# Modulation columns by a multiply-and-sum over weights with features on partitions, and the first input made tile by tile

## The chip, the cores and the metric

The program runs on one core of a Trainium2 chip. Its time is device microseconds from start to end of one execution; the median of three runs before the change is 1673.4 us (1672.69 to 1673.78). TensorE is PE, VectorE DVE, ScalarE ACT, GpSimd POOL, and SyncE (SP) issues most transfers.

## The reference, cut to what matters

Two transformer-like models run one after the other over one sequence of 256 tokens with 1024 features, all in float32. The first has two layers whose normalised input is scaled and shifted by a modulation made of one conditioning vector c. For each layer six vectors of 1024 features are computed:

```
s      = silu(c)                       # 1024 values
mod[v] = s @ w_ada[:, v] + b_ada[v]    # v = 0..5, each 1024 features
v = 0, 1: shift and scale of the mixer's input
v = 3, 4: shift and scale of the feed-forward's input
v = 2, 5: gate of the branch's result (added as 1 + mod[v])
h      = x * (1 + scale) + shift
```

The input of the first mixer is `x * (1 + mod[1]) + mod[0]`, without a norm. From it q, k and v of two kinds of heads are projected, attention is computed, its result projected by w_o, gated, added and normalised; a gated feed-forward follows; then layer two, and then the second model (two more layers, which the change does not touch).

## The kernel before, in words

All weights are streamed from HBM in tiles of 128 x 1024 floats (512 KB) by SP's queue, in program order. `load` (L224) puts a tile into one of four "raw" buffers and splits it into two float32r parts: ACT casts the high part (L230), VectorE subtracts to get the low part (L239). Each product is three matmuls: high x high, high x low, low x high (`tok`, L260, for a 128-token block; `feat`, L249, and `both`, L305, for features).

w_ada tiles go into four buffers "ra" of their own. A step of `ada_acc` (L606) loads one tile of 128 input features x 1024 output features and adds it, times the 128 values of silu(c) as a per-partition scalar, to an accumulator "acc" (L618, L620). After eight steps acc holds on each partition a part of every output feature's sum. For gate rows (`ada_row`) a matmul with ones sums over partitions and leaves the row on all of them (L647). For shift and scale the features must lie on partitions: `ada_cols` (L627) runs eight matmuls with one column each, acc as the stationary operand (L632, 16 records in the profile), and one small VectorE instruction adds the bias (L633). The steps stand in a list "background", of which one or so is taken out with each `load`, so that they lie between the weights of the mixer and the feed-forward.

The first input has its own code at the start. `first_half` (L800) loads eight tiles that hold 512 features of shift and of scale, sums them on VectorE (L808, L810), runs the eight one-column matmuls (L813), and adds the biases (L815, L816). `first_hT` (L818) makes the four hT tiles of that half (L823 on ACT, L825 on VectorE, split at L243 and L244), and `first_v` (L828) projects them to v with weights v_ab; for these loads every second low part is subtracted by POOL. Then the second half does the same. The four results are copied out of PSUM by VectorE (L854). The order within an engine's queue is chosen when the program is built, from the program order and a scheduler's estimates; each engine runs its queue in that order.

Of the kernel before, what the change touches and what calls it, by code (L numbers as in the profile page):

```python
# [37 lines left out]
LAMBDA_INIT = 0.8 - 0.6 * math.exp(-0.3 * 0)  # L38
TWO_PI = 2.0 * math.pi
# [70 lines left out]
def tile_two_blocks(ctx: ExitStack, tc: tile.TileContext, d: dict, out: bass.AP, upto: int = 99):  # L110
# [489 lines left out]
    with ExitStack() as b1:  # L600
        b1.enter_context(extra_w(XW))
        adap = b1.enter_context(tc.tile_pool(name="adap", bufs=2))
        sc = keep.tile([P, 8], F32, name="sc")
        A.activation(sc, pc("c"), AF.Silu)

        def ada_acc(l, v, then):  # L606
# [3 lines left out]
            def step(k):  # L610
                if k == 0:
                    box.append(adap.tile([P, 1024], F32, tag="acc", name=nm("acc"), bufs=ACCB))
                acc = box[0]
                raw = adap.tile([P, 1024], F32, tag="ra", name=nm("ra"), bufs=RAB)
                last_dma[0] = nc.sync.dma_start(raw, d["w_ada"][l, k, :, v * D:(v + 1) * D])
                with tc.issue_after(last_norm[0].ins) if last_norm[0] else nullcontext():
                    if k == 0:
                        V.tensor_scalar(acc, raw, sc[:, 0:1], None, op0=ALU.mult)  # L618
                    else:
                        V.scalar_tensor_tensor(acc, in0=raw, scalar=sc[:, k:k + 1], in1=acc, op0=ALU.mult, op1=ALU.add)  # L620
                if k == KT - 1:
                    then(acc)
# [177 lines left out]
        def first_half(h, gain, bias):  # L800

            acc = adap.tile([P, 1024], F32, tag="acc", name=nm("acc"), bufs=ACCB)
            for k in range(KT):
                raw = adap.tile([P, 1024], F32, tag="ra", name=nm("ra"), bufs=RAB)
                last_dma[0] = nc.sync.dma_start(
                    raw.rearrange("p (v c) -> p v c", v=2), d["w_ada"][0, k, :, 0:2 * D].rearrange("p (v c) -> p v c", v=2)[:, :, h * 512:(h + 1) * 512])
                if k == 0:
                    V.tensor_scalar(acc, raw, sc[:, 0:1], None, op0=ALU.mult)  # L808
                else:
                    V.scalar_tensor_tensor(acc, in0=raw, scalar=sc[:, k:k + 1], in1=acc, op0=ALU.mult, op1=ALU.add)  # L810
            b = pbank()
            for k in range(KT):
                mm(b[:, k:k + 1], acc[:, k * P:(k + 1) * P], cc("ones")[:, 0:1], start=True, stop=True)  # L813
            c = slice(4 * h, 4 * h + 4)
            V.scalar_tensor_tensor(gain[:, c], in0=b[:, 4:8], scalar=1.0, in1=pc("b_ada", 8 + 4 * h, 4), op0=ALU.add, op1=ALU.add)  # L815
            V.tensor_add(bias[:, c], b[:, 0:4], pc("b_ada", 4 * h, 4))  # L816

        def first_hT(h, xb, hT, gain, bias):  # L818
            for k in range(4 * h, 4 * h + 4):
                i = xb[k // 2][:, (k % 2) * T:(k % 2 + 1) * T]  # L820
                z = np_.tile([P, T], F32, tag="pr", name=nm("h"), bufs=3)
                if k % 2 == 0:
                    A.activation(z, i, AF.Identity, scale=gain[:, k:k + 1], bias=bias[:, k:k + 1])  # L823
                else:
                    V.tensor_scalar(z, i, gain[:, k:k + 1], bias[:, k:k + 1], op0=ALU.mult, op1=ALU.add)  # L825
                split(hT[:, 0, k, :], hT[:, 1, k, :], z)

        def first_v(h, ws, vb, hT):  # L828
            for t in range(2):
                for k in range(4 * h, 4 * h + 4):  # L830
                    tok(vb[t], ws[k // 2 - 2 * h], (k % 2) * 512, hT, k, t, first=k == 0, last=k == KT - 1)
# [3 lines left out]
        gain, bias = keep.tile([P, 8], F32, name="gain"), keep.tile([P, 8], F32, name="bias")  # L835
        pool_share[1] = 0.5
# [5 lines left out]
        for h in range(2):  # L842
            first_half(h, gain, bias)
            first_hT(h, xb, hT, gain, bias)
            if h == 0:
                vab = [[pbank(), pbank()], [bank(), bank()]]
            with tc.issue_after(last_dma[0].ins):
                ws = [[load(d["v_ab"][j][2 * h + i]) for i in range(2)] for j in range(2)]
# [720 lines left out]
def layout(a):  # L1569
# [38 lines left out]
    def inter(q, k):  # L1608
# [4 lines left out]
        "w_ada": a["w_ada"].reshape(2, KT, P, 6 * D), "b_ada": a["b_ada"], "ln_g": a["ln_g"], "ln_b": a["ln_b"],  # L1613
# [47 lines left out]
```

## Time and profile before

| what | value |
|---|---|
| median of three runs | 1673.4 us |
| profiled execution, its own time | 1672.3 us |
| span of the trace within it | 1670.5 us |
| TensorE busy, matmul / weight load | 1609.5 us / 1357.5 us |
| VectorE, ACT, POOL busy | 1254.5, 899.4, 129.7 us |
| one-column matmul records: L813, L632 | 32, 96 |
| mean granted TensorE clock | 0.991 of full speed |

Busy times of matmuls overlap and their ends are modelled, so a full TensorE row says that it had work in hand, and not that it ran at its peak. The chain of waits goes back from the last instruction, at each step to what released it; its pieces in a stretch show which work set the time there. The granted clock of a stretch is 1.00 at 2.4 GHz and 0.50 at 1.2 GHz.

### The profile page before, as it was taken

The page shows a single profiled execution, that of the slowest core. Times are in us where ns is not written, and L with a number is a line of the kernel's source. Part 1 is how long each engine was busy: PE and PEld are TensorE (multiplying, and loading weights), DVE is VectorE, ACT ScalarE, POOL GpSimd, SP SyncE. Part 2 cuts the span into 40 slices and gives each one's busy share as a digit, 9 for nine tenths or more (in the row PEclk, how much of TensorE's full clock was granted, in tenths as well). Part 3 has the DMA queues.
Part 4 walks back from the last instruction along what each step waited for, and adds up shares of the span by engine and source line. Part 5 has one row for each costly group of instructions (what it writes and reads, how often), then busy time and mean ns, then how long its engine had stood idle before and what let it go on. Part 6 is the DMA issues. An engine that isn't in the chain of part 4 may idle for free.

```text
span 1670.5 us, 24925 instructions
## 1 busy us (share of the span) xinstructions
PE 1609.5 (96%) x9156; PEld 1357.5 (81%) x9156; DVE 1254.5 (75%) x2468; ACT 899.4 (54%) x1650; POOL 129.7 (8%) x170
## 2 busy tenths in 40 slices
PE   5899999999999999899999999999999999999998
PEld 4787788878877888688887878888888887778887
DVE  6898988989769766897766897766676667666663
ACT  2465654556446545445556566555565555655552
POOL 1110000000000000286100100000000002000000
PEclk9899999999989999999999999999999999999999
DMA  8877788848726655245554336655375555545550
GB/s 283 333 281 259 242 309 313 310 163 290 253 88 235 235 186 189 98 169 177 193 191 154 118 124 222 234 189 189 124 231 192 192 182 164 177 139 202 190 190 37
DMA packets 103210, 336.14 MB, mean 201 GB/s; under 512 B 15008, under 2 KB 20384, under 8 KB 103088
## 3 DMA queue, kind: packets, MB, share of 16 engines
q1 hardware_dynamic: 102368, 332.54, 57.6%
q10 hardware_dynamic: 720, 2.02, 0.3%
q8 instruction: 71, 1.16, 0.3%
q14 instruction: 51, 0.42, 0.1%
HBM read 332.41 MB, written 2.10 MB: 200 GB/s over the span
## 4 chain that ended last, share of the span: by engine, by line
PE 80%; DVE 10%; DMA 3%; ACT 3%; issue 1%; POOL 1%; SPq 0%; POOLq 0%; ACTq 0%; DVEq 0%
PE p L309 26%; PE p L311 14%; PE a L336 7%; PE a L337 7%; PE a L338 7%; DVE wt L239 3%; PE p L264 3%; PE p L266 3%; PE p L265 2%; PE a L172 2%; PE qk L256 2%; PE qk L257 2%; PE qk L258 2%; ACT wt L230 1%; PE a L479 1%
## 5 line engine op out<-in xcount | busy, mean ns | idle before, releaser
L239 DVE TENSOR_TENSOR wt<-raw,wt 128x512 fp32r<-128x512 f32 (+1 forms) x940 | 675.8, 747 | 146.3 <-ACT wt L230 140.4
L230 ACT CAST wt<-raw 128x1024 fp32r<-128x1024 f32 x512 | 535.9, 1049 | 228.9 <-PE a L338 90.9
L309 PE MATMUL p<-hT,wt 128*128 128x512 f32 x1920 | 484.1, 393 | 0.0
L309 PEld LDWEIGHTS p<-hT,wt 128*128 128x128 f32 x1920 | 352.0, 189 | 68.5 <-issue 1.2
L311 PEld LDWEIGHTS p<-hT,wt 128*128 128x128 f32 x1920 | 262.7, 191 | 18.6 <-issue 0.2
L311 PE MATMUL p<-hT,wt 128*128 128x256 f32 x1920 | 269.3, 283 | 0.0
L336 PE MATMUL a<-wt,r 128*128 128x512 f32 x528 | 206.9, 392 | 0.0
L337 PE MATMUL a<-wt,r 128*128 128x512 f32 x528 | 206.8, 392 | 0.0
L338 PE MATMUL a<-wt,r 128*128 128x512 f32 x528 | 206.1, 390 | 0.0
L264 PE MATMUL p<-wt,hT 128*128 128x512 f32 x352 | 143.8, 411 | 6.1 <-ACT hT L243 5.1
L266 PE MATMUL p<-wt,hT 128*128 128x512 f32 x352 | 141.5, 404 | 2.6 <-DVE hT L244 2.5
L265 PE MATMUL p<-wt,hT 128*128 128x512 f32 x352 | 141.3, 403 | 2.4 <-DVE wt L239 1.5
L315 ACT COPY s<-p 128x256 f32<-128x256 f32 x120 | 44.5, 371 | 165.2 <-PE p L311 165.1
L338 PEld LDWEIGHTS a<-wt,r 128*128 128x128 f32 x528 | 99.2, 188 | 21.4 <-DVE r L244 0.3
L336 PEld LDWEIGHTS a<-wt,r 128*128 128x128 f32 x528 | 99.6, 189 | 18.0
L337 PEld LDWEIGHTS a<-wt,r 128*128 128x128 f32 x528 | 99.5, 189 | 17.1
L315 ACT COPY pr<-p 128x256 f32<-128x256 f32 x120 | 44.5, 371 | 107.9 <-PE p L311 107.8
L316 DVE TENSOR_TENSOR s<-p,s 128x256 f32<-128x256 f32 x120 | 50.8, 423 | 65.9 <-ACT s L315 65.4
L256 PE MATMUL qk<-hT,wt 128*128 128x256 f32 x320 | 94.3, 295 | 0.0
L257 PE MATMUL qk<-hT,wt 128*128 128x256 f32 x320 | 92.9, 290 | 0.0
L258 PE MATMUL qk<-hT,wt 128*128 128x256 f32 x320 | 92.8, 290 | 0.0
L620 DVE SCALAR_TENSOR_TENSOR acc<-ra,sc,acc 128x1024 f32<-128x1024 f32 x70 | 89.3, 1276 | 0.0
(335 smaller groups left out, 1838.4 us busy)
## 6 DMA issues: line engine op xcount, KB each, us to landing
raw<-in_w_ffn_d_dram SPq DMA_DIRECT2D x132, 512.0 KB, 3.3
raw<-in_w_ffn_g_dram SPq DMA_DIRECT2D x120, 512.0 KB, 3.3
raw<-in_w_ffn_u_dram SPq DMA_DIRECT2D x120, 512.0 KB, 3.3
ra<-in_w_ada_dram SPq DMA_DIRECT2D x96, 512.0 KB, 5.2
raw<-in_w_ffn_dram SPq DMA_DIRECT2D x24, 512.0 KB, 3.6
raw<-in_w_ab_dram SPq DMA_DIRECT2D x16, 512.0 KB, 5.6
raw<-in_w_o_dram SPq DMA_DIRECT2D x16, 512.0 KB, 5.4
raw<-in_w_cd_dram SPq DMA_DIRECT2D x16, 512.0 KB, 4.4
```

What stands on the lines that cost most here:

```text
L230: A.copy(w[:, 0, :n], raw[:, :n])
L239: last_part[eng is G] = eng.tensor_sub(w[:, 1, c:c + g], raw[:, c:c + g], w[:, 0, c:c + g])
L256: mm(o, wh, xh, start=first and k == 0, stop=False)
L257: mm(o, wh, xl, start=False, stop=False)
L264: mm(o, xh, w[:, 0, c0:c0 + n], start=first, stop=False)
L265: mm(o, xh, w[:, 1, c0:c0 + n], start=False, stop=False)
L266: last_tok[0] = mm(o, xl, w[:, 0, c0:c0 + n], start=False, stop=last)
L309: mm(o, w[:, 0, k * P:(k + 1) * P], both_parts, start=k == 0, stop=False)
L311: mm(o[:, T:2 * T], w[:, 1, k * P:(k + 1) * P], hT[:, 0, k, :], start=False, stop=k == KT - 1)
L336: mm(o, a[:, 0, tt_(t)], w[:, 0, c], start=m == 0, stop=False)
L337: mm(o, a[:, 0, tt_(t)], w[:, 1, c], start=False, stop=False)
L338: mm(o, a[:, 1, tt_(t)], w[:, 0, c], start=False, stop=m == MT - 1)
```

## The change

silu(c) is also kept as a row "crow": c is read with one transfer to all 128 partitions, and ACT applies Silu over 1024 elements. The host lays the w_ada tiles for shift and scale out with output features on partitions and all 1024 input features along the row. One VectorE instruction (tensor_tensor_reduce) multiplies such a tile by crow, in place, and sums along the row: 128 finished features in one column. `ada_cols` needs no accumulator and no matmul, `ada_row` is as before but for its source's layout. The start goes through the eight feature tiles in order: two sums, one addition of biases, one ACT instruction, cast and subtraction, and after each pair of tiles the matmuls of both v projections, whose weights are now loaded two at a time ahead of the w_ada tiles. POOL subtracts nothing at the start, all four v banks come from one PSUM pool, and ACT copies the results out.

```diff
+        crow = adap.tile([P, 1024], F32, tag="crow", name="crow", bufs=1)
+        nc.scalar.dma_start(crow, d["c_row"].to_broadcast([P, D]))
         A.activation(sc, pc("c"), AF.Silu)
+        A.activation(crow, crow, AF.Silu)
...
+        def ada_dot(l, v, f, o):
+            raw = adap.tile([P, 1024], F32, tag="ra", name=nm("ra"), bufs=RAB)
+            last_dma[0] = nc.sync.dma_start(raw, d["w_ada_col"][l, COLV.index(v), f])
+            with tc.issue_after(last_norm[0].ins) if last_norm[0] else nullcontext():
+                V.tensor_tensor_reduce(raw, raw, crow, 1.0, 0.0, ALU.mult, ALU.add, o)
+
         def ada_cols(l, v, o, plus=0.0):
-            def then(acc):
-                b = pbank()
-                for k in range(KT):
-                    mm(b[:, k:k + 1], acc[:, k * P:(k + 1) * P], cc("ones")[:, 0:1], start=True, stop=True)
-                V.scalar_tensor_tensor(o, in0=b[:, 0:8], scalar=plus, in1=pc("b_ada", (l * 6 + v) * 8, 8),
-                                       op0=ALU.add, op1=ALU.add)
-            ada_acc(l, v, then)
+            def step(f):
+                ada_dot(l, v, f, o[:, f:f + 1])
+                if f == KT - 1:
+                    V.scalar_tensor_tensor(o, in0=o, scalar=plus, in1=pc("b_ada", (l * 6 + v) * 8, 8),
+                                           op0=ALU.add, op1=ALU.add)
+            for f in range(KT):
+                background.append(lambda f=f: step(f))
...
+        def first_hT(k, xb, hT, mod_):
+            for v in range(2):
+                with tc.issue_after(last_dma[0].ins) if last_dma[0] else nullcontext():
+                    ada_dot(0, v, k, mod_[:, v, k:k + 1])
+            V.tensor_add(mod_[:, :, k:k + 1], mod_[:, :, k:k + 1], b01[:, :, k:k + 1])
+            z = np_.tile([P, T], F32, tag="pr", name=nm("h"), bufs=3)
+            A.activation(z, xb[k // 2][:, (k % 2) * T:(k % 2 + 1) * T], AF.Identity,
+                         scale=mod_[:, 1, k:k + 1], bias=mod_[:, 0, k:k + 1])
+            split(hT[:, 0, k, :], hT[:, 1, k, :], z)
...
-        pool_share[1] = 0.5
...
+        vab = [[pbank(), pbank()], [pbank(), pbank()]]
+        for h in range(KT // 2):
+            with tc.issue_after(last_dma[0].ins) if last_dma[0] else nullcontext():
+                ws = [load(d["v_ab"][j][h]) for j in range(2)]
+            for k in (2 * h, 2 * h + 1):
+                first_hT(k, xb, hT, mod_)
             for j in range(2):
-                first_v(h, ws[j], vab[j], hT)
+                for t in range(2):
+                    for k in (2 * h, 2 * h + 1):
+                        tok(vab[j][t], ws[j], (k % 2) * 512, hT, k, t, first=k == 0, last=k == KT - 1)
         for j in range(2):
             for t in range(2):
                 v = kept()
-                V.tensor_copy(v, vab[j][t])
+                A.copy(v, vab[j][t])
```

Three places show how instructions move. The first is VectorE's queue at the start, before, from the last sums of the first half to its first hT (acc: accumulator, ra and raw: weight buffers, wt: split weights):

```order
L810 SCALAR_TENSOR_TENSOR acc_132<-ra_148,sc,acc_132 128x1024
L691 TENSOR_SCALAR mlam<-s_99 128x1
L810 SCALAR_TENSOR_TENSOR acc_132<-ra_151,sc,acc_132 128x1024
L810 SCALAR_TENSOR_TENSOR acc_132<-ra_154,sc,acc_132 128x1024
L815 SCALAR_TENSOR_TENSOR gain<-p_157,prm 128x4
L816 TENSOR_TENSOR bias<-p_157,prm 128x4
L239 TENSOR_TENSOR wt_190<-raw_188,wt_190 128x1024
L244 TENSOR_TENSOR hT_109<-h_168,hT_109 128x256
L825 TENSOR_SCALAR h_172<-a_112,gain,bias 128x256
L825 TENSOR_SCALAR h_180<-a_113,gain,bias 128x256
```

and after, from the second multiply-and-sum on (it stands as two ISA rows, the second of which reads the sum; crow: silu(c) as a row, mod: finished columns, b: biases):

```order
L638 ISA ra_154,mod_114<-ra_154,crow 128x1024
L638 ISA mod_114 128x1
L704 TENSOR_SCALAR mlam<-s_102 128x1
L638 ISA ra_162,mod_114<-ra_162,crow 128x1024
L638 ISA mod_114 128x1
L818 TENSOR_TENSOR mod_114<-mod_114,b_113 128x2
L638 ISA ra_165,mod_114<-ra_165,crow 128x1024
L638 ISA mod_114 128x1
L246 TENSOR_TENSOR hT_112<-h_158,hT_112 128x256
L818 TENSOR_TENSOR mod_114<-mod_114,b_113 128x2
L241 TENSOR_TENSOR wt_199<-raw_197,wt_199 128x1024
L246 TENSOR_TENSOR hT_112<-h_169,hT_112 128x256
```

The first hT subtraction stood behind eight steps over a whole half, and now stands behind four sums and two weight subtractions; the later weight subtractions stand between the sums of the next tiles.

The second is ACT's queue at the start, which also issues transfers (prm: columns of parameters, cst: constants, sc: silu(c) as columns, g: lambda's row). Before:

```order
L150 DMA prm<-in_cols_dram 128x348
L152 DMA cst<-in_consts_dram 128x1284
L155 DMA x<-in_x_dram 128x1024 x2
L604 ACT_TABLE_LOAD
L604 ACTIVATE sc<-prm 128x8
L682 DMA g_96<-in_lam_dram 128x256
L1050 ACT_TABLE_LOAD
L1050 ACTIVATE s_7013<-prm 128x16
L688 ACTIVATE s_98<-s_98 128x2
L230 CAST wt_190<-raw_188 128x1024
L823 ACTIVATE h_168<-a_112,bias,gain 128x256
```

and after:

```order
L152 DMA prm<-in_cols_dram 128x348
L154 DMA cst<-in_consts_dram 128x1284
L157 DMA x<-in_x_dram 128x1024 x2
L608 DMA crow<-in_c_row_dram 128x1024
L609 ACT_TABLE_LOAD
L609 ACTIVATE sc<-prm 128x8
L695 DMA g_99<-in_lam_dram 128x256
L610 ACTIVATE crow<-crow 128x1024
L232 CAST wt_143<-raw_141 128x1024
L232 CAST wt_148<-raw_146 128x1024
```

crow's transfer stands behind x and ahead of lambda's, and its Silu ahead of the first weight cast.

The third is TensorE's queue in the feed-forward of layer one, around a modulation column's matmuls (p: PSUM banks of gate and up, a: those of the down projection, r: the gated activations). Before:

```order
L309 MATMUL p_2617<-hT_1375,wt_2612 128x512 x8
L311 MATMUL p_2617<-hT_1375,wt_2612 128x256 x8
L632 MATMUL p_2664<-cst,acc_2414 128x1 x8
L336 MATMUL a_1833<-wt_2676,r_2577 128x512
L337 MATMUL a_1833<-wt_2676,r_2577 128x512
```

and after:

```order
L311 MATMUL p_2585<-hT_1353,wt_2580 128x512 x8
L313 MATMUL p_2585<-hT_1353,wt_2580 128x256 x8
L338 MATMUL a_1802<-wt_2635,r_2545 128x512
L339 MATMUL a_1802<-wt_2635,r_2545 128x512
L340 MATMUL a_1802<-wt_2635,r_2545 128x512
```

The group on acc is gone, and the matmuls of the down projection follow the gate and up at once.

## Rows read from the trace of the kernel before

**Rows 1.** page, parts 1 and 4: busy us (share) xinstructions; shares of the chain

```profile
PE 1609.5 (96%) x9156; PEld 1357.5 (81%) x9156; DVE 1254.5 (75%) x2468; ACT 899.4 (54%) x1650; POOL 129.7 (8%) x170
...
PE 80%; DVE 10%; DMA 3%; ACT 3%; issue 1%; POOL 1%; SPq 0%; POOLq 0%; ACTq 0%; DVEq 0%
```

**Rows 2.** busy by stage: PE, PEld, DVE, ACT, POOL, granted clock, DMA share, GB/s

```profile
0.00:66.40 66.40, 37.88 (x146) 30.92 (x147) 44.02 (x55) 18.74 (x29) 11.18 (x8) 0.92 0.83 297
66.40:113.00 46.60, 45.87 (x363) 41.68 (x362) 43.91 (x108) 27.17 (x72) 3.98 (x3) 1.00 0.84 306
113.00:190.00 77.00, 75.78 (x437) 60.03 (x436) 69.91 (x163) 48.10 (x112) 3.41 (x3) 1.00 0.74 253
190.00:360.00 170.00, 169.58 (x900) 144.77 (x899) 146.12 (x251) 87.39 (x147) 0.95 (x1) 1.00 0.81 286
```

**Rows 3.** chain of waits, 0 to 120 us: start, us, what

```profile
2.24 12.95 DMA ra<-in_w_ada_dram
...
22.00 3.58 PE p L813 x16
...
66.14 0.23 PE a L266
```

**Rows 4.** the same in short stretches

```profile
4.00:6.00 2.00, 0.00 (x0) 0.00 (x0) 0.66 (x4) 1.06 (x3) 0.00 (x0) 1.00 1.06 416
...
32.00:34.00 2.00, 1.74 (x8) 1.10 (x6) 2.00 (x2) 0.00 (x0) 2.00 (x1) 1.00 0.00 0
...
46.00:48.00 2.00, 1.19 (x6) 1.19 (x6) 0.76 (x1) 1.04 (x1) 0.00 (x0) 0.50 1.03 422
...
56.00:58.00 2.00, 2.00 (x10) 1.41 (x8) 2.00 (x2) 0.93 (x1) 1.94 (x1) 1.00 0.88 296
...
476.00:477.00 1.00, 1.00 (x4) 0.73 (x3) 0.26 (x4) 0.47 (x2) 0.00 (x0) 0.50 0.00 0
```

**Rows 5.** timeline, VectorE, 73.9 to 78 us: start, duration, engine, line, operation

```profile
73.96 0.29 DVE L493 CUSTOM_DVE_ANT_0 g<-a,g 128x128 f32<-128x128 f32 x1 [1.01 <-PE a L479]
...
74.18 0.42 DVE L493 CUSTOM_DVE_ANT_0 g<-a,g 128x256 f32<-128x256 f32 x1
74.53 0.09 DVE L493 DVE_READ_ACCUMULATOR2_ANT s<- 128x1 f32 x1
74.53 1.22 DVE L239 TENSOR_TENSOR wt<-raw,wt 128x1024 fp32r<-128x1024 f32 x1
75.66 0.16 DVE L496 RECIPROCAL s<-s 128x2 f32<-128x2 f32 x1
...
76.28 1.28 DVE L620 SCALAR_TENSOR_TENSOR acc<-ra,sc,acc 128x1024 f32<-128x1024 f32 x1
77.48 0.16 DVE L496 RECIPROCAL s<-s 128x2 f32<-128x2 f32 x1
```

**Rows 6.** VectorE's groups by line and form: xcount | busy, mean ns

```profile
L244 DVE TENSOR_TENSOR hT<-h,hT 128x256 fp32r<-128x256 f32 x8 | 10.3, 1303 | 0.0
...
L618 DVE TENSOR_SCALAR acc<-ra,sc 128x1024 f32<-128x1024 f32 x10 | 7.4, 744 | 0.0
```

**Rows 7.** timeline, all engines, start of the program

```profile
14.37 0.36 DVE L686 TENSOR_TENSOR g<-g 128x64 f32<-128x64 f32 x2 [0.48 <-DMA g<-in_lam_dram]
...
21.81 1.04 ACT L230 CAST wt<-raw 128x1024 fp32r<-128x1024 f32 x1 [4.81 <-DMA raw<-in_v_ab_dram]
...
25.94 0.56 ACT L823 ACTIVATE h<-a,bias,gain 128x256 f32<-128x256 f32 x1 [3.09 <-DVE bias L816]
...
26.97 0.43 DVE L244 TENSOR_TENSOR hT<-h,hT 128x256 fp32r<-128x256 f32 x1
...
46.81 3.57 PE L813 MATMUL p<-cst,acc 128*128 128x1 f32 x16 [5.26 <-DVE acc L810]
```

**Rows 8.** chain of waits: first and last of the six L632 groups

```profile
119.64 1.68 PE p L632 x16
...
470.60 2.27 PE p L632 x16
```

More of the change, by code (lines that the diff above doesn't have):

```diff
@@ L38 @@
 LAMBDA_INIT = 0.8 - 0.6 * math.exp(-0.3 * 0)
+COLV = (0, 1, 3, 4)
 TWO_PI = 2.0 * math.pi
@@ L614, in step @@
                 raw = adap.tile([P, 1024], F32, tag="ra", name=nm("ra"), bufs=RAB)
-                last_dma[0] = nc.sync.dma_start(raw, d["w_ada"][l, k, :, v * D:(v + 1) * D])
+                last_dma[0] = nc.sync.dma_start(raw, d["w_ada_row"][l, v // 3, k])
                 with tc.issue_after(last_norm[0].ins) if last_norm[0] else nullcontext():
@@ L798, in log1p @@
             V.tensor_sub(o, o, e)
[L800 to L831, printed above, removed]
+        def first_hT(k, xb, hT, mod_):
[7 more added lines that the diff above has]
+            split(hT[:, 0, k, :], hT[:, 1, k, :], z)
@@ L834, in tile_two_blocks @@
         hT = new_hT()
-        gain, bias = keep.tile([P, 8], F32, name="gain"), keep.tile([P, 8], F32, name="bias")
-        pool_share[1] = 0.5
+        b01, mod_ = (keep.tile([P, 2, 8], F32, name=n) for n in ("b01", "mod01"))
+        V.tensor_copy(b01[:, 0, :], pc("b_ada", 0, 8))
+        V.tensor_scalar(b01[:, 1, :], pc("b_ada", 8, 8), 1.0, None, op0=ALU.add)
         xb = [bank() for _ in range(4)]
@@ L841, in tile_two_blocks @@
                 transpose(xb[k // 2][:, o:o + P], x[:, t, k * P:(k + 1) * P])
[L842 to L848, printed above, removed]
+        vab = [[pbank(), pbank()], [pbank(), pbank()]]
[4 more added lines that the diff above has]
+                first_hT(k, xb, hT, mod_)
             for j in range(2):
-                first_v(h, ws[j], vab[j], hT)
+                for t in range(2):
+                    for k in (2 * h, 2 * h + 1):
+                        tok(vab[j][t], ws[j], (k % 2) * 512, hT, k, t, first=k == 0, last=k == KT - 1)
         for j in range(2):
@@ L1552, in _tok, with _ada @@
     return np.ascontiguousarray(w.reshape(4, 2, P, 512).transpose(0, 2, 1, 3)).reshape(4, P, 1024)
+def _ada(w, vs):
+    return np.ascontiguousarray(w.reshape(2, KT, P, 6, D).transpose(0, 3, 1, 2, 4)[:, list(vs)])
 def _first(g, u):
@@ L1612, in layout @@
         "consts": consts, "sel": sel, "band": band, "cols": cols, "x": a["x"].reshape(2, P, D),
-        "w_ada": a["w_ada"].reshape(2, KT, P, 6 * D), "b_ada": a["b_ada"], "ln_g": a["ln_g"], "ln_b": a["ln_b"],
+        "c_row": a["c"].reshape(1, D), "w_ada_row": _ada(a["w_ada"], (2, 5)),
+        "w_ada_col": np.ascontiguousarray(_ada(a["w_ada"], COLV).reshape(2, 4, D, KT, P).transpose(0, 1, 3, 4, 2)), "b_ada": a["b_ada"], "ln_g": a["ln_g"], "ln_b": a["ln_b"],
         "rel": rel, "lam": a["diff_lambda"].reshape(1, 256),
```

## Prediction, made before the changed kernel ran

> **What bounds the kernel now.** I read the page's busy shares and chain first, then the stages, then the start in small pieces. The page shows TensorE busy 96% of the span and carrying 80% of the chain that ended last; VectorE carries 10% [rows 1]. The stages show where TensorE isn't full: up to 66.4 us it is busy only 37.88 us, and behind that it is busy nearly all the time, 45.87 of 46.60, 75.78 of 77.00, 169.58 of 170.00 us, with VectorE almost as full in the first of these (43.91 of 46.60) [rows 2]. So two questions decide: how early the first projection (v_ab) ends, and which TensorE work goes away behind it.
>
> The chain of the start shows why TensorE waits: 12.95 us for first weights of w_ada, then VectorE sums, then 16 one-column matmul records of L813 (3.58 us), and all of this again for the second half of the features (46.81 us, [rows 7]); the last matmul of the v projection ends at 66.14 + 0.23 = 66.4 us [rows 3]. The transfers don't run through: 416 GB/s at 4 to 6 us, nothing at 32 to 34 us, when the four buffers "ra" wait for VectorE and the four "raw" for the second half. The second half runs at a granted clock of 0.50 (1.2 GHz) after TensorE had idled 5.26 us [rows 7], and only at 56 us is it back at 1.00 (2.4 GHz) [rows 4].
>
> **The start, step by step.** Both L813 groups, both waits for a whole half and the four POOL subtractions go. In their place each of the 8 feature tiles needs two 512 KB tiles and two multiply-and-sum instructions; then one small addition, one ACT instruction, a cast and a subtraction give that tile's hT. Bytes stay the same but for crow (512 KB). What is late next is VectorE, in order:
>
> - Cost of a multiply-and-sum over 1024 elements: not in the trace, but the same instruction exists in the softmax (L493). 128 elements start 0.22 us before the next instruction (73.96 to 74.18), 256 elements 0.35 us (74.18 to 74.53), so 0.13 us per 128 columns: 0.35 + 6 × 0.13 = 1.13 us. The reading of its sum starts with the next instruction, at the same 74.53. The nearest whole row, scalar_tensor_tensor over 1024, takes a step of 1.20 us (76.28 to 77.48) [rows 5]. I take 1.20; from above 1.28 + 0.08 = 1.36, if the reading stood alone.
> - VectorE's list for the start is 16 × 1.20 = 19.2 us; 8 weight subtractions of 1.13 (74.53 to 75.66) [rows 5] = 9.0; 8 hT subtractions of 0.43 [rows 7] = 3.4 (the 1.30 us mean of this form in the start [rows 6] holds those that ran beside POOL's subtractions, and POOL has none now); 8 additions of 0.15 = 1.2; lambda and the like 1.4; the first ada_row step 0.74 [rows 6]. Sum 35.0 us.
> - It begins when crow is there. crow stands on ACT's queue behind prm, cst and x (1.88 MB) and ahead of lam. lam, the last 0.13 MB of 2.01 MB on that queue, was used at 14.37 us [rows 7], while SP's queue was full beside it. crow is the last of 2.41 MB; 0.40 MB more at half of 0.4 MB/us is 2.0 us: 16.4 us. Its Silu over 1024 elements at the 1.04 us of a cast [rows 7] ends at 17.4.
> - 17.4 + 35.0 = 52.4 us for the last hT. TensorE then has the 12 matmuls of the last tile: 12 × 0.23 [rows 3] = 2.8 us at 2.4 GHz, about twice that at 1.2 GHz. In between it idles 2 to 3.5 us per pair of tiles (some 8 us of VectorE against 24 × 0.23 = 5.5 us of matmuls), less than the 5.26 us ahead of the fall [rows 7], so I put the end nearer to full clock, at 55.5. Gain 66.4 − 55.5 = 10.9 us.
>
> From both sides: transfers alone need 15.1 MB (2.4 on ACT, 12.6 on SP) at 0.416 MB/us from 2.4 us on, 38.7 us; sum, addition and ACT to hT (25.94 to 27.40, 1.46 us [rows 7]) and 2.8 us make 44.3, a gain of 22. From above: crow 6 us later (all its partitions read one row of HBM; lam does so too, and nothing shows its rate apart), sums at 1.36 (+2.6), end at half clock (57.6): 66.2, a gain of nothing.
>
> The four copies of v move from VectorE to ACT; there they stand behind the first w_ab cast (1.04 [rows 7]), and the first q/k matmul now also needs a bank that the first copy frees. I cost this at nothing: the 12 last matmuls (2.8 us) hide a cast and a copy of half its size; if the cast comes late, the q/k matmul waits for it anyway. Without that cover it costs about 1 us.
>
> The Trainium skill (DMA: Bandwidth & Descriptors, Specifications) puts HBM at about 358 GB/s per core; by it the transfers alone would end at 44.6 instead of 38.7 us, and the best case would be a gain of 16, not 22. The 416 GB/s of 4 to 6 us say otherwise [rows 4].
>
> **Behind the start.** The other six columns (mod of both layers) lose a group of 16 matmul records each (L632): six pieces of the chain, 1.68 us for the first, 2.27 for the last, 10.8 us in all [rows 8]. TensorE has nothing beside them, and they stand in stages in which it is full [rows 2], so I count all of it. VectorE pays 8 × 1.20 + 0.17 instead of 0.74 + 7 × 1.20 + 0.17, 0.46 us more per column, 2.7 in all, and gets back its own waits for these matmuls; it has 2.7, 7.1 and 23.9 us idle in the three stages, which hide this. Without cover it costs 2.7. The queue order of SP around these columns only shifts by a place or two. Bounds: 3.4 us, if only the two groups in the feed-forward pay, up to 14.1, if the 6.6 us at 0.50 that follow the last group (476 to 477 is one row of it [rows 4]) run at full clock too, 3.3 us saved.
>
> Sum against the profiled execution (1672.3 us): 1672.3 − 10.9 − 10.8 = 1650.6. That execution lies 1.1 us under the median of the runs, so 1651.7, or **1652 us**.
>
> **Rivals.**
> 1. VectorE, not TensorE, limits the two mixers, so that taking matmuls away there gives nothing. For it: VectorE is busy 94% and 91% of the two stages. Against: TensorE's waits in them are small, 0.73 and 1.22 us. Time: 1673.4 − 10.9 − 3.4 = 1659 us. The Trainium skill points the same way (Perfetto Trace Analysis, Identifying the Most-Contended Engine): matmul busy time is not to be trusted, weight loads are. By it, weight loads at 41.68 of 46.60 and 60.03 of 77.00 us put VectorE first in both stages [rows 2]. The chain, which names the groups themselves, speaks against it [rows 8].
> 2. crow and the buffers are late, and the start gains only 3 us. For it: four "ra" buffers, refilled only as VectorE frees them, behind v_ab transfers in one queue. Against: 8 transfers stand ready at once, and a slot has a cycle of some 8 us to come back. Time: 1673.4 − 3 − 10.8 = 1660.
> 3. The start comes near its transfers and the clock stays up: gains of 16 and 13 us, 1644.
> 4. Slower: the multiply-and-sum over 1024 elements of SBUF takes two passes, some 2.4 us. Place: 16 in the start, all on the path (+19), and 16 in the first mixer, where 10 us of VectorE's idle time take half (+9); 28 − 21.7 gives 1680. It decides from about 2.2 us per instruction on. Against: the softmax's slope of one column in about 1 ns [rows 5]; its input is in PSUM, though, so it isn't excluded.
> 5. What goes is given back by another order of the mixers' instructions: 1673.
>
> **How the numbers follow.** The forecast has 0.52, rival 1 0.16, rival 2 0.14, rival 3 0.10, rival 4 0.05, rival 5 0.03. The range reaches over rivals 1 and 2 with a little for both together, and to rival 3: 1643 to 1665. 0.2% is 3.3 us, what a measurement of this kernel can tell: faster 0.92, same 0.03, slower 0.05.
>
> **What would show it.** In the profile after: no L632 and L813 groups; multiply-and-sum rows of about 1.25 us with a reading of 0.08 beside the next; the first of them near 17.5 us, and VectorE without long gaps from there to 52; no POOL work; the last v matmul near 55.5; the stages behind it each shorter by their groups, 1.7 us apiece. I am wrong if the sums take over 1.5 us, if the first starts past 20, if TensorE waits more in the mixers than before, or if the clock falls between the feature tiles.

## The result, and the profile after

The changed kernel takes 1649.4 us (median of 4 runs, 1649.22 to 1651.59), the kernel before 1673.05 us beside it (4 runs, 1672.51 to 1673.78). The ratio is 0.9858, 95% interval 0.9843 to 0.9872: 23.7 us faster, 2.6 us under the forecast and inside its range. The profiled execution after took 1649.22 us, with a span of 1647.2 us.

The page after, parts 1 and 4 (busy us, share, instructions; shares of the chain that ended last), beside [rows 1]:

```profile
PE 1587.3 (96%) x9028; PEld 1334.8 (81%) x9028; DVE 1248.9 (76%) x2534; ACT 905.6 (55%) x1659; POOL 119.0 (7%) x166
...
PE 78%; DVE 12%; ACT 3%; DMA 3%; issue 2%; POOL 1%; SPq 0%; ACTq 0%; POOLq 0%; DVEq 0%
```

128 TensorE records are gone (32 of L813, 96 of L632) and 22.2 us of its busy time. VectorE's share of the chain rises from 10 to 12%, its busy time does not.

Fixed stages as in [rows 2] don't tell where the time came from, since the work has slid against them. So both traces are cut at the same pieces of work: the first q/k matmul, the first down-projection matmul of the first feed-forward (L338 after, L336 before), the 401st q/k matmul record (the 17th of the second mixer), the 397th record of that down-projection line (halfway through the second feed-forward), the end. Columns: stretch, length, busy time of PE, PEld, DVE, ACT, POOL, granted clock, DMA share, GB/s. The kernel before:

```profile
0.00:66.21 66.21, 37.69 (x145) 30.73 (x145) 43.92 (x55) 18.69 (x28) 11.18 (x8) 0.92 0.83 297
66.21:186.09 119.88, 117.92 (x782) 98.68 (x781) 110.24 (x266) 73.02 (x180) 7.38 (x6) 1.00 0.78 273
186.09:376.53 190.44, 189.05 (x995) 160.47 (x994) 165.60 (x289) 101.10 (x176) 1.50 (x2) 1.00 0.77 272
376.53:607.91 231.38, 228.44 (x1329) 191.92 (x1328) 183.89 (x423) 129.19 (x257) 1.59 (x2) 0.97 0.63 218
607.91:1670.50 1062.59, 1036.38 (x5914) 875.73 (x5912) 750.87 (x1439) 577.37 (x1009) 108.07 (x152) 1.00 0.50 171
```

The kernel after, cut at the same work:

```profile
0.00:56.97 56.97, 30.06 (x112) 23.13 (x113) 36.55 (x73) 22.07 (x34) 0.20 (x4) 0.97 0.87 322
56.97:174.91 117.94, 114.90 (x750) 95.04 (x748) 110.41 (x281) 75.55 (x183) 7.34 (x6) 1.00 0.80 293
174.91:361.40 186.49, 185.28 (x963) 156.94 (x962) 166.16 (x305) 101.00 (x177) 1.10 (x2) 1.00 0.78 278
361.40:586.32 224.92, 221.77 (x1298) 185.88 (x1297) 184.05 (x439) 129.59 (x257) 1.86 (x2) 0.98 0.65 224
586.32:1647.20 1060.88, 1035.30 (x5914) 873.85 (x5912) 751.71 (x1439) 577.36 (x1009) 108.55 (x152) 1.00 0.52 171
```

Read the lengths: the start gives 9.24 us, the next three stages, each of which held two groups of one-column matmuls (32 records; the counts after lack 32, 32 and 31, since a record that lies across a cut counts on both sides), 1.94, 3.95 and 6.46 us, and the rest of the program, where nothing was changed, 1.71 us. Together 23.3, the difference of the spans.

In the start, VectorE's timeline after (start, duration, engine, line, operation, idle time before it and its releaser) shows the new instruction, to be laid beside [rows 5]:

```profile
17.43 1.23 DVE L638 CUSTOM_DVE_ANT_0 ra<-ra,crow 128x1024 f32<-128x1024 f32 x1 [11.86 <-ACT crow L610]
...
28.07 1.22 DVE L638 CUSTOM_DVE_ANT_0 ra<-ra,crow 128x1024 f32<-128x1024 f32 x1
29.21 0.08 DVE L638 DVE_READ_ACCUMULATOR2_ANT mod<- 128x1 f32 x1
29.21 1.22 DVE L638 CUSTOM_DVE_ANT_0 ra<-ra,crow 128x1024 f32<-128x1024 f32 x1
30.36 0.08 DVE L638 DVE_READ_ACCUMULATOR2_ANT mod<- 128x1 f32 x1
...
51.62 0.43 DVE L246 TENSOR_TENSOR hT<-h,hT 128x256 fp32r<-128x256 f32 x1 [0.40 <-ACT hT L245]
```

A sum over 1024 elements starts 1.14 to 1.15 us before what follows it, and the reading of the sum lies beside the next one. The first begins at 17.43 us, the last hT at 51.62 us.

TensorE's timeline after, from the last pair of feature tiles to the first q/k matmul:

```profile
50.08 0.79 PE L266 MATMUL p<-wt,hT 128*128 128x512 f32 x1 [2.85 <-ACT hT L245]
50.67 0.63 PE L267 MATMUL p<-wt,hT 128*128 128x512 f32 x1
51.10 0.63 PE L266 MATMUL p<-wt,hT 128*128 128x512 f32 x1
...
53.34 0.39 PE L268 MATMUL p<-wt,hT 128*128 128x512 f32 x1
53.57 0.39 PE L266 MATMUL p<-wt,hT 128*128 128x512 f32 x1
...
56.97 0.28 PE L258 MATMUL qk<-hT,wt 128*128 128x256 f32 x1
```

All 24 matmuls of the pair are still to do at 50.08 us. The first start 0.43 us apart, the later ones 0.23: the clock fell in the 2.85 us in which TensorE waited, and rose again before 54 us. Busy times in short stretches, same columns as above:

```profile
48.00:50.00 2.00, 0.00 (x0) 0.00 (x0) 2.00 (x4) 0.94 (x2) 0.00 (x0) 0.88 0.97 354
50.00:52.00 2.00, 1.92 (x5) 1.54 (x6) 1.60 (x6) 0.99 (x3) 0.00 (x0) 0.50 0.76 223
52.00:54.00 2.00, 2.00 (x8) 1.62 (x7) 0.97 (x2) 1.05 (x1) 0.00 (x0) 0.76 0.96 379
```

The time lost to the clock can be summed from such rows: 2 us times (1 − granted clock), here 0.24 + 1.00 + 0.48 = 1.7 us. Done for every 2 us of both traces (up to 1640 us), the kernel before loses 5.1 us in the start, 6.8 in its fourth stage and 3.4 behind it, the kernel after 1.7, 3.4 and 1.7. So at most 8.5 of the 23.3 us are clock; in the start it is less than the 3.4 of the sums, because TensorE waited in a part of the low stretch ([rows 4], 46 to 48 us: 1.19 of 2.00 busy).

### The profile page after: what moved, and what is told of

Its sections match the earlier page's. It is cut to its first block, busy times and chain, and to the rows that moved or that the text cites. A ratio compares the mean times of both kernels' runs of the same rounds, so it can differ in the third digit from the quotient of the medians.

```text
span 1647.2 us, 24708 instructions
## 1 busy us (share of the span) xinstructions
PE 1587.3 (96%) x9028; PEld 1334.8 (81%) x9028; DVE 1248.9 (76%) x2534; ACT 905.6 (55%) x1659; POOL 119.0 (7%) x166
## 3 DMA queue, kind: packets, MB, share of 16 engines
q8 instruction: 70, 1.15, 0.3%
## 4 chain that ended last, share of the span: by engine, by line
PE 78%; DVE 12%; ACT 3%; DMA 3%; issue 2%; POOL 1%; SPq 0%; ACTq 0%; POOLq 0%; DVEq 0%
PE p L311 26%; PE p L313 14%; PE a L338 7%; PE a L339 7%; PE a L340 7%; DVE wt L241 4%; PE p L266 3%; PE p L268 3%; PE p L267 3%; PE a L174 2%; ACT wt L232 1%; PE qk L260 1%; PE qk L258 1%; PE qk L259 1%; DVE ra L638 1%
## 5 line engine op out<-in xcount | busy, mean ns | idle before, releaser
L338 PE MATMUL a<-wt,r 128*128 128x512 f32 x528 | 206.8, 392 | 0.2 <-ACT r L245 0.2
L266 PE MATMUL p<-wt,hT 128*128 128x512 f32 x368 | 149.5, 409 | 17.6 <-ACT hT L245 16.5
L267 PE MATMUL p<-wt,hT 128*128 128x512 f32 x368 | 147.0, 400 | 2.1 <-DVE wt L241 2.0
L268 PE MATMUL p<-wt,hT 128*128 128x512 f32 x368 | 146.4, 401 | 0.4 <-DVE hT L246 0.2
L338 PEld LDWEIGHTS a<-wt,r 128*128 128x128 f32 x528 | 99.5, 188 | 18.5 <-ACT r L245 0.4
L266 PEld LDWEIGHTS p<-wt,hT 128*128 128x128 f32 x368 | 70.4, 192 | 39.4 <-ACT hT L245 21.2
```

The costliest lines, as they stand in the source:

```text
L266: mm(o, xh, w[:, 0, c0:c0 + n], start=first, stop=False)
L267: mm(o, xh, w[:, 1, c0:c0 + n], start=False, stop=False)
L268: last_tok[0] = mm(o, xl, w[:, 0, c0:c0 + n], start=False, stop=last)
L338: mm(o, a[:, 0, tt_(t)], w[:, 0, c], start=m == 0, stop=False)
```

## The experiments

Each kernel ran on the same chip as the kernels sent with it and the kernel before. Since the times of one kernel spread by 3 to 9 us there, what is said of a place in the program is read from the traces. All were cut at the same five pieces of work as above. Lengths in us; the last column is the time lost to the clock, in the start / the fourth stage / behind it (the second and third lose none in any run):

| kernel | start | 2nd | 3rd | 4th | rest | span | clock |
|---|---|---|---|---|---|---|---|
| before | 66.2 | 119.9 | 190.4 | 231.4 | 1062.6 | 1670.5 | 5.1 / 6.8 / 3.4 |
| after | 57.0 | 117.9 | 186.5 | 224.9 | 1060.9 | 1647.2 | 1.7 / 3.4 / 1.7 |
| after, run again | 56.3 | 118.0 | 186.5 | 223.0 | 1060.9 | 1644.6 | 6.8 / 1.7 / 5.1 |
| new start only | 57.7 | 120.7 | 190.3 | 233.5 | 1060.7 | 1663.0 | 3.4 / 6.8 / 1.7 |
| new columns only | 66.5 | 118.3 | 187.3 | 224.5 | 1063.2 | 1659.8 | 6.8 / 3.4 / 3.4 |
| groups put back | 55.0 | 120.8 | 190.1 | 231.5 | 1062.6 | 1660.0 | 0 / 6.8 / 3.4 |
| row of c first | 55.5 | 118.0 | 186.5 | 225.4 | 1059.0 | 1644.4 | 1.7 / 3.4 / 1.7 |
| more on VectorE | 64.5 | 114.4 | 186.7 | 224.8 | 1063.7 | 1654.0 | 3.4 / 3.4 / 5.1 |
| both rows first | 53.1 | 118.0 | 186.5 | 224.9 | 1061.4 | 1643.9 | 1.7 / 3.4 / 3.4 |
| the same, filled | 52.5 | 117.9 | 186.5 | 225.6 | 1062.5 | 1645.0 | 0 / 3.4 / 3.4 |
| copies on VectorE | 55.8 | 118.3 | 186.7 | 226.4 | 1062.3 | 1649.5 | 1.7 / 5.1 / 3.4 |
| weights second | 52.6 | 118.0 | 186.7 | 226.7 | 1062.0 | 1645.9 | 3.4 / 5.1 / 3.4 |
| the same, filled | 51.0 | 117.9 | 186.7 | 225.0 | 1060.0 | 1640.5 | 1.7 / 3.4 / 1.7 |

The unaltered kernel was run again as a measure:

> The changed kernel itself, unaltered, as the measure for the three runs beside it on one chip. 1649 us, ratio to the kernel before 0.986, first q/k matmul at 57 us.

Measured: 1648.87 us (4 runs), ratio 0.9853 [0.9836, 0.9869], first q/k matmul at 56.30 us. Its two traces differ by 2.65 us of span: that is how far one profile of a kernel can stand from another. The third stage, without low clock, repeats within 0.01 us. The start repeats less well: the four traces with the same start (after, run again, new start only, groups put back) have the first q/k matmul at 57.0, 56.3, 57.7 and 55.0 us. In all four TensorE begins the last pair's 24 matmuls at 49.1 to 50.1 us; they differ by the low clock behind that. Nor is the sum of the last column a price: run again, the kernel loses 13.6 us to the clock instead of 6.8, and its span is shorter.

**Start and columns apart.** One kernel with the new start and the old columns:

```diff
-            def step(f):
-                ada_dot(l, v, f, o[:, f:f + 1])
...
+            def then(acc):
+                b = pbank()
+                for k in range(KT):
+                    mm(b[:, k:k + 1], acc[:, k * P:(k + 1) * P], cc("ones")[:, 0:1], start=True, stop=True)
...
+            ada_acc(l, v, then)
```

> The start as in the changed kernel (feature tile by feature tile, sums on VectorE), the other six modulation columns as before: VectorE accumulators and one-column matmuls with ones. Theory (the two gains are separate and add up): only the start's gain is left, 9.2 us at the first q/k matmul, so 1673 - 9 = 1664 us, and the six groups of one-column matmuls are back in the chain. Rival (VectorE limits the mixers, the six groups cost nothing there; nearly all of the gain is the start): 1650 to 1655 us.

and one with the old start (first_half, L813, POOL's share, as in the kernel before) and the new columns:

> The start as before (two halves of the features, POOL's share, one-column matmuls), the other six modulation columns by multiply-and-sum. Theory: the six groups of one-column matmuls were on the path and go, 10.8 us by the chain of before, up to 14 with the low clock behind the last one; so 1659 to 1662 us, and together with the run of the start alone the two gains add up to the whole 23.6 us within 2 us. Rival (VectorE limits the mixers): 1669 to 1673 us.

Measured: 1663.94 us (5 runs), ratio 0.9945 [0.9928, 0.9962], and 1663.13 us (4 runs), ratio 0.9938 [0.9915, 0.9962], beside 1673.73 us (8 runs). Gains of 9.8 and 10.6 us: both rivals are out. The first is what its theory said, the second falls 1 us short of its 1659 to 1662, and the two add up to 20.4 of the 23 to 24 us, 3 us short where 2 were allowed for; the intervals (3 and 4 us to each side) leave room for the whole. Which part of the new start gives how much (no L813 groups, pairs of tiles instead of halves, no subtractions on POOL) no run separates. The stages agree: the new start alone leaves the second and third stage where they were or 0.8 us longer. Its fourth stage is 2.2 us longer than before at the same loss to the clock, because of a wait at 386 to 396 us for an instruction of VectorE, L533 (2.30 us up to 391.83), which eight other traces show shorter, 0.5 to 1.4 us:

```profile
386.00:390.00 4.00, 3.54 (x30) 3.33 (x28) 4.00 (x11) 1.94 (x4) 0.00 (x0) 1.00 0.55 181
390.00:396.00 6.00, 4.17 (x25) 4.16 (x26) 6.00 (x16) 4.02 (x10) 0.00 (x0) 0.77 0.86 290
```

TensorE is idle 2.29 of these 10 us, and VectorE is full. Why its work piles up there isn't settled.

**The groups alone.** The sums stay, and behind each column's last one the 16 records come back, on data at hand, read by nobody:

```diff
                 if f == KT - 1:
+                    b = pbank()
+                    for k in range(KT):
+                        mm(b[:, k:k + 1], crow[:, k * P:(k + 1) * P], cc("ones")[:, 0:1], start=True, stop=True)
```

> The changed kernel, with a group of 8 one-column matmuls (16 records) added behind the last sum of each of the six later columns, on data at hand; nobody reads their result, so VectorE doesn't wait for them. Theory (TensorE is full in these stages and the groups alone were the cost): 6 x 1.7 to 2.3 us back, 10 to 13 us more, 1659 to 1662 us. Rival (VectorE limits the mixers; what was gained there is that VectorE no longer waits for the groups): only the two groups in the feed-forward cost, 3 to 4 us, 1653 us.

Measured: 1662.6 us (6 runs), ratio 0.9933 [0.9914, 0.9951] to the kernel before, where the changed kernel run again has 0.9853: 0.0080 of 1673.85 us, about 13.4 us (4 to each side), is lost again, the upper end of what the theory said and far from the rival's 3 to 4. VectorE doesn't wait for these groups, and they cost all the same: the time was TensorE's. In the second and third stage TensorE runs its other matmuls in the same order as after, so nothing else of its work has moved there. The stages of this trace, second to fourth:

```profile
54.98:175.81 120.83, 118.54 (x782) 98.57 (x781) 111.29 (x282) 75.53 (x183) 7.33 (x6) 1.00 0.80 290
175.81:365.94 190.13, 188.94 (x995) 160.51 (x994) 167.12 (x305) 101.58 (x177) 1.10 (x2) 1.00 0.76 273
365.94:597.39 231.45, 228.28 (x1329) 191.82 (x1328) 184.01 (x439) 129.44 (x257) 1.59 (x2) 0.97 0.63 218
```

They are 2.89, 3.64 and 6.53 us longer than after, 13.1 in all. The fourth has 3.4 us more low clock than after, so its two groups themselves are worth some 3.1. Where the low clock lies shows in short stretches of the same trace; the last group starts at 460.00 and takes 2.42 us:

```profile
460.00:462.00 2.00, 2.00 (x17) 2.00 (x15) 1.50 (x8) 1.52 (x7) 0.00 (x0) 0.82 0.81 245
462.00:464.00 2.00, 2.00 (x7) 1.65 (x7) 1.41 (x12) 0.09 (x1) 0.00 (x0) 0.50 0.06 22
464.00:466.00 2.00, 2.00 (x7) 1.55 (x6) 0.00 (x0) 0.48 (x1) 0.00 (x0) 0.50 0.00 0
466.00:468.00 2.00, 2.00 (x6) 1.17 (x5) 0.00 (x0) 0.00 (x0) 0.00 (x0) 0.50 0.00 0
```

In the kernel before the same follows its last group (470.60 us, [rows 8]):

```profile
472.00:474.00 2.00, 2.00 (x8) 1.81 (x8) 1.09 (x7) 0.49 (x2) 0.00 (x0) 0.50 0.33 126
474.00:476.00 2.00, 2.00 (x7) 1.50 (x7) 1.93 (x16) 0.71 (x3) 0.00 (x0) 0.50 0.00 0
```

The new start with old columns shows it too (group at 464.76, 0.96 from 464 to 465, 0.50 up to 470). In all three kernels with these groups the fourth stage loses 6.8 us to the clock, in the ten traces without them 1.7 to 5.1, in seven of these 3.4. That the group makes the clock fall isn't shown, though: the fall lies at its start or within it, and in the kernel after, which has no group there, the clock falls at the same piece of work:

```profile
452.00:454.00 2.00, 2.00 (x11) 1.39 (x8) 1.24 (x8) 1.60 (x8) 0.00 (x0) 0.58 0.72 240
454.00:456.00 2.00, 2.00 (x8) 1.64 (x7) 1.63 (x13) 0.81 (x3) 0.00 (x0) 0.57 0.24 92
```

Three more of the ten traces without groups show the same. This stretch loses 1.7 us, the one at the group 3.4; the rest of the difference lies at other places. What the groups cost in clock stays open.

**What sets the start.** First, more work on VectorE, which nobody uses:

```diff
+            return raw
...
-                    ada_dot(0, v, k, mod_[:, v, k:k + 1])
+                    raw = ada_dot(0, v, k, mod_[:, v, k:k + 1])
+                    V.tensor_mul(raw[:, 0:512], raw[:, 0:512], crow[:, 0:512])
```

> The changed kernel, with one extra VectorE multiplication over 512 columns behind each of the 16 sums of the start (about 0.6 us each, its result is not used). Theory (VectorE's list is the path of the start): 16 x 0.6 = 9.6 us later, about 1659 us, and VectorE without gaps up to about 61 us. Rival (the transfers set the start): VectorE's idle time swallows most of it, 1650 to 1653 us.

Measured: 1651.81 us (4 runs), ratio 0.9876 [0.9858, 0.9895]. By the end time the rival seems right, by the place the theory: each multiplication takes 0.60 us, 16 are 9.6 us, and the first q/k matmul comes 7.5 us later, at 64.52.

```profile
0.00:64.52 64.52, 32.56 (x113) 23.74 (x113) 47.91 (x91) 22.70 (x35) 0.20 (x4) 0.95 0.82 308
64.52:178.88 114.36, 112.65 (x750) 95.00 (x749) 107.97 (x280) 76.00 (x185) 7.46 (x6) 1.00 0.80 290
```

VectorE is full from 20 to 60 us. But the stage behind it is 3.6 us shorter than after (114.36 against 117.94): TensorE waits 1.7 us in it instead of 3.0, and is busy 112.65 us instead of 114.90 with the same records. They don't come in the same order, though: of the 748 matmuls counted from the first q/k, 387 places hold another one than after. So the 3.6 us can't be put down to VectorE, which has 107.97 us of work there instead of 110.41; what shortens the stage isn't shown. This trace is also that of the longest of the four executions (1655.94 us, the others 1651.42 to 1652.05), so the 7.5 us and the median don't belong together.

Next, the row of c first on ACT's queue, ahead of constants and x:

```diff
         nc.scalar.dma_start(crow, d["c_row"].to_broadcast([P, D]))
+        nc.scalar.dma_start(prm, d["cols"])
+        nc.scalar.dma_start(cst, d["consts"])
...
+        A.activation(crow, crow, AF.Silu)
         A.activation(sc, pc("c"), AF.Silu)
-        A.activation(crow, crow, AF.Silu)
```

> The changed kernel, with the broadcast row of c put first on ACT's queue, ahead of the constants and x, and its Silu ahead of the small one. Theory (the start is VectorE's list of 35 us, which begins when the row is there, at 17.4 us): the row lands 5 to 8 us earlier, VectorE begins at about 10 to 12 us, and the end comes 4 to 6 us earlier, 1644 to 1646 us. Rival (transfers set the start: the first projection waits for weights that come behind one another in the queue): VectorE begins earlier but waits for tiles later, about 1 us is gained, 1648 to 1649 us.

Measured: 1648.44 us (4 runs), ratio 0.9853 [0.9833, 0.9874], no different from the changed kernel; first q/k at 55.45, within the 55.0 to 57.7 of the unaltered start. The theory's first half holds, its second not: the time is the rival's. VectorE's timeline:

```profile
10.92 1.22 DVE L638 CUSTOM_DVE_ANT_0 ra<-ra,crow 128x1024 f32<-128x1024 f32 x1 [2.17 <-DMA ra<-in_w_ada_col_dram]
...
13.31 1.23 DVE L638 CUSTOM_DVE_ANT_0 ra<-ra,crow 128x1024 f32<-128x1024 f32 x1 [1.16 <-DMA ra<-in_w_ada_col_dram]
...
18.15 0.36 DVE L699 TENSOR_TENSOR g<-g 128x64 f32<-128x64 f32 x2 [3.60 <-DMA g<-in_lam_dram]
```

The list begins 6.5 us earlier and is then stopped by a small instruction that stands third in it and wants lambda's row, the last transfer of its queue. So that row was put forward too:

```diff
+        lam = slot()
         nc.scalar.dma_start(crow, d["c_row"].to_broadcast([P, D]))
+        nc.scalar.dma_start(lam[:, 0:256], d["lam"].to_broadcast([P, 256]))
```

> The changed kernel with two transfers put first on ACT's queue: the broadcast row of c, then the row for lambda. With the row of c alone in front, VectorE did two sums by 14.5 us and then stood 3.6 us until lambda's row landed, since its instructions run in order. Theory (the start is VectorE's list, which then runs from about 11 us): the 3.6 us go, the first q/k matmul is at 52 us instead of 57, 1644 us. Rival (weights of the projection come behind the w_ada tiles in one queue, and tile buffers come free one by one): VectorE is stopped at other tiles, and q/k starts no earlier than 54.5 us, 1647 us.

Measured: 1645.84 us (5 runs), ratio 0.9834 [0.982, 0.9847], first q/k at 53.06 us. Between the two: 3.2 us earlier than the same chip's 56.30, not 5, and 1.9 earlier than the earliest of the unaltered starts. VectorE begins at 9.99 us and then stops at other things, as the rival said:

```profile
9.99 1.22 DVE L640 CUSTOM_DVE_ANT_0 ra<-ra,crow 128x1024 f32<-128x1024 f32 x1
...
13.06 1.22 DVE L640 CUSTOM_DVE_ANT_0 ra<-ra,crow 128x1024 f32<-128x1024 f32 x1 [1.84 <-DMA ra<-in_w_ada_col_dram]
...
15.57 1.23 DVE L640 CUSTOM_DVE_ANT_0 ra<-ra,crow 128x1024 f32<-128x1024 f32 x1 [1.20 <-DMA ra<-in_w_ada_col_dram]
...
21.98 0.43 DVE L242 TENSOR_TENSOR hT<-h,hT 128x256 fp32r<-128x256 f32 x1 [1.63 <-ACT hT L241]
```

The last is ACT's order: its first h stood behind the casts of the second pair's weights. Loading each pair's weights between its two tiles changes that:

```diff
+            first_hT(2 * h, xb, hT, mod_)
...
                 ws = [load(d["v_ab"][j][h]) for j in range(2)]
-            for k in (2 * h, 2 * h + 1):
-                first_hT(k, xb, hT, mod_)
+            first_hT(2 * h + 1, xb, hT, mod_)
```

> The run with both rows first, with the two weight tiles of each pair loaded between its two feature tiles instead of ahead of both. There the first h on ACT stood behind the casts of the second pair's weights, whose transfer was issued only at 11.8 us (VectorE idle 1.63 us ahead of the first hT, besides 3 us for tiles). Theory (these are what is left of the start): first hT at 17 to 19 us instead of 22, first q/k at 50 to 51 us instead of 53, 1643 us. Rival (tiles just come later in one queue, the sum of bytes sets it): within 1 us of the run it is made from, 1645 to 1647 us.

Measured: 1644.42 us (4 runs), ratio 0.9825 [0.9804, 0.9846]. The first hT comes at 18.73 us, as expected, and the first q/k at 52.60, only 0.5 us earlier, so the rival is nearer: VectorE now waits 3.04 us for a tile at 15.47, and 3.4 us are lost to the clock. By the time the two can't be told apart.

**The clock at the start's end.** Matmuls that nobody reads, in time in which TensorE would wait; 8 behind each of the first three pairs, added to the kernel with both rows first:

```diff
+            if h < 3:
+                z = bank()
+                for i in range(8):
+                    mm(z, hT[:, 0, 2 * h, 0:P], ws[1][:, 0, 0:512], start=True, stop=True)
```

> The run with both rows first, and 8 matmuls of 512 columns behind each of the first three pairs of feature tiles, into a bank that nobody reads (8 x 0.23 us, in time in which TensorE would wait). Theory (the clock falls because TensorE waits between the pairs): the granted clock stays at 1.00 up to the first q/k matmul and 1 to 2 us are gained against the run without them. Rival (the fall has another cause, or the added matmuls push the real ones back): the clock falls as before and the time is the same or up to 2 us more.

Measured: 1645.88 us (4 runs), ratio 0.983 [0.9815, 0.9845]. The granted clock stays at 1.00 up to the first q/k. That the filling did it isn't shown: with the groups put back, where nothing fills, TensorE waits 2.87 us ahead of the last pair and the start loses nothing to the clock either. Short stretches of the kernel without them:

```profile
46.00:48.00 2.00, 2.00 (x7) 1.58 (x8) 1.53 (x4) 0.97 (x2) 0.00 (x0) 0.69 0.75 234
48.00:50.00 2.00, 2.00 (x6) 1.53 (x5) 0.04 (x1) 1.05 (x1) 0.00 (x0) 0.50 0.99 383
```

The same stretches with them:

```profile
46.00:48.00 2.00, 2.00 (x11) 1.65 (x10) 1.44 (x4) 0.97 (x2) 0.00 (x0) 1.00 0.89 307
48.00:50.00 2.00, 2.00 (x10) 1.68 (x9) 0.00 (x0) 0.77 (x1) 0.00 (x0) 1.00 1.01 370
```

But q/k starts only 0.5 us earlier (52.52): 24 more matmuls of 0.23 us, 5.5 us, fill TensorE, so the rest of the rival holds too. With 3 behind each pair, and the weights second:

> The same with 3 matmuls of 512 columns that nobody reads behind each of the first three pairs. With 8 of them the granted clock stayed at 1.00 to the end of the start, but TensorE was full with them from 22 to 52 us and the gain was 0.5 us. Theory: 3 are enough to keep the clock and don't fill TensorE, 1 to 2 us less than without them, 1642 us. Rival (the clock falls as before, or the last hT sets the end): no difference.

Measured: 1646.36 us (4 runs), ratio 0.9831 [0.981, 0.9852]. The first q/k is at 51.01, 1.6 us earlier than without them, with one low stretch, at 40 to 44 us, instead of two, at 31 to 35 and 48 to 52; the time doesn't tell them apart.

**The four copies of v** back on VectorE:

```diff
-                A.copy(v, vab[j][t])
+                V.tensor_copy(v, vab[j][t])
```

> The changed kernel with the four copies of v back on VectorE instead of ACT. The prediction put this move at nothing, at 1 us without cover. Theory (the place of the copies costs nothing): within 1 us of the changed kernel. Rival (VectorE is the fuller engine here: 4 x 0.7 us of copies hold back its work for the first heads): 1 to 3 us more, at the first mixer.

Measured: 1650.51 us (4 runs), ratio 0.9858 [0.9844, 0.9871], against 0.9853 [0.9836, 0.9869]: 1.6 us more by the medians, as the rival has it, but no difference that the intervals can tell. The second stage, where VectorE would pay, is 0.4 us longer.

The four versions with both rows first have the lowest ratios to the kernel before, 0.9825 to 0.9834, beside 0.9853 and 0.9858 of the changed kernel: some 3 to 5 us, much as at the first q/k matmul. Their intervals just overlap the changed kernel's, and among the four nothing can be told apart by the time.

## Why the prediction was right

- **VectorE is late next.** Shown: more work on it moves the first q/k by 7.5 of 9.6 us. A list that begins 7.4 us earlier moves it by less than half of that (3.2), since VectorE then waits for tiles and for ACT. The list itself was right within half a microsecond: predicted 17.4 to 52.4, traced 17.43 to 52.05 (51.62 + 0.43). The sums were 16 × 0.06 = 1.0 us cheaper than the 1.20 taken; the lower end worked out from the softmax, 1.13, was nearly exact. Additions and hT subtractions were cheaper too; waits of 1.7 us in all took most of that back.
- **crow at 17.4 us**: right, though I didn't see what made it late. I went by lambda's row in the kernel before and the bytes that crow has more. The chain after shows that the transfer was issued only at 5.12 us, behind the landing of an earlier one, and then took 11.19 us, to 16.3. Lambda's had been held in the same way (issued at 5.24 us, 9.1 us to landing), so the difference, 2.1 us for my 2.0, came out:

```profile
0.73 4.37 DMA prm<-in_cols_dram
5.12 11.19 DMA crow<-in_c_row_dram
16.34 1.06 ACT crow L610
```

- **End of the start**: predicted 55.5, measured 57.0 (55.0 to 57.7 over the four traces), so 9.2 us instead of 10.9. The failing term is the 2.8 us behind the last hT; from 52.05 it took 4.9. I let the tiles come evenly, with 12 matmuls left behind the last. In fact the four sums of a pair run together and its two hT come 1.56 us apart (50.06 and 51.62), so that all 24 matmuls remained at 50.08: 5.5 us at 2.4 GHz, and the clock, which I took as nearly full, added 1.5 (the rows from 50 to 54 us): 57.1. The trace with the groups put back, whose clock stayed at 1.00, has 5.6 us for them (49.41 to 54.98). (At half clock the prediction's own terms end the start at 58.0, not at the 57.6 of its upper bound; nothing hangs on it.)
- **The six groups**: predicted 10.8 us at full price. The three stages gave 1.94 + 3.95 + 6.46 = 12.35, and putting the groups back took 13.1. The third stage is the cleanest, with TensorE's order the same in all kernels and no low clock: its pair gave 3.95 and took 3.64, against 3.4 on the chain. In the fourth, 3.4 of the 6.46 us are low clock, which I had only in the upper bound (14.1), and which the groups aren't shown to cause. In the first mixer the pair gave 1.9 instead of 3.5, though putting it back cost 2.9. There the order of TensorE's matmuls changed, of which my sum had nothing: 251 of the 748 places behind the first q/k hold another matmul than before. Twice the scores now follow their q and k so closely that TensorE waits 0.44 us for ACT's copy of these; first the kernel before, then the one after:

```profile
73.01 0.93 PE L479 MATMUL a<-qks 64*128 64x128 f32 x8
...
63.59 0.93 PE L481 MATMUL a<-qks 64*128 64x128 f32 x8 [0.44 <-ACT qks L569]
```

TensorE's waits for ACT in this stage rise from 0.2 to 1.1 us, those for VectorE only from 1.7 to 1.8. The new start with the old columns has the two waits as well, and its second stage is 0.8 us longer than before.
- **Signs of being wrong**: two of the four came up, at a small size. TensorE waits more in the first mixer than before (3.0 us against 2.0), and the clock fell ahead of the last pair of tiles.
- **Rival 1** is refuted as a whole by the groups put back, and has a small part in the first mixer. The Trainium skill (Perfetto Trace Analysis, Identifying the Most-Contended Engine) would have VectorE first there, by weight loads of 95.04 of 117.94 us after against VectorE's 110.41. The measured 2.89 us for groups that VectorE doesn't wait for say that TensorE's time counted. Its small part is the 0.6 us that are missing to the groups' 3.5: with the groups TensorE waits 1.2 us for VectorE, without them 1.8. With the old start and the new columns it waits 4.0 us for VectorE in this stage.
- **Rival 2** (crow and buffers late): crow is late, and 3 to 4 us lie in it, but the gain of the start stood. **Rival 3** didn't come: the clock fell, and the start ended at 57.0 us. **Rival 4** is out at 1.14 us per sum. **Rival 5** is out as a whole by the stages, and has a small part in the first mixer, about 0.9 us.
- **The sum** was nearer than its terms: the start gave 1.7 less, the groups 1.6 more, and 1.71 us came in stages where nothing was changed, which no step of mine had. By the table this goes with the clock: traces that lose 1.7 us there take 1059.0 to 1060.9 us, those that lose 3.4 take 1061.4 to 1063.2; only the kernel run again, with 5.1 and 1060.9, doesn't fit.

## What to carry to other kernels

When the list of an engine sets a stage, find what starts it: an operand far back in a queue held 16 large instructions, and when it came early, the next operand behind it did. Count what is left behind the last arrival in the units in which the code groups its work, here a pair of tiles and not one. Matmuls of one column cost their own time in a stage where TensorE is full: price them by putting them back without their consumers. Before a stage that got longer or shorter is put down to an engine or to the clock, see whether the order in the queue is the same, and look at the same piece of work in traces without the change.

## What the runs showed of the hardware

- The low stretches of TensorE's clock lie at places that shift between two runs of one kernel: one trace of the changed kernel loses 1.7, 3.4 and 1.7 us in the three parts of the table, the other 6.8, 1.7 and 5.1. The sum alone tells little: with 5.1 us more of it in the start, the second trace has its first q/k 0.7 us earlier. In the fourth stage, where TensorE is full, 1.7 us less of it went with 1.9 us less time.
- The clock was at 0.50 behind the last group of one-column matmuls in all three kernels that have it, while TensorE was counted busy 2.00 of 2.00 us; in four of the ten traces without the group it fell at the same piece of work.
- A transfer can be held at its issue, not only in its queue: in the changed kernel crow's was issued at 5.12 us, right behind prm's landing at 5.10. With crow first, Silu began at 7.75 us instead of 16.34, and lambda's row was the one held, issued at 11.09 behind the constants' landing. The rule behind this wasn't tested.
- One core moved 418 GB/s over the 9.4 us behind the start (57.00 to 66.40 us after), more than the 358 GB/s that the Trainium skill (DMA: Bandwidth & Descriptors, Specifications) gives per core, as half of what the memory of two cores moves.
